# Sixty-four transposes in an attention layer: from TensorE to DMA on planes of 16 bits

## The chip, the cores and the metric

The kernel runs on one core of a Trainium2 chip. Its engines are called PE (TensorE, matrix products), ACT (ScalarE), DVE (VectorE), POOL (GpSimd) and SP (SyncE, which here only issues DMAs). The metric is the device time of one execution in microseconds (us); lower is better.

## The reference

One layer of an encoder on 256 tokens of width 2048: a normalisation, one input projection, two attention branches, sigmoid gates that mix them, an output projection and an MLP. Only the attention and the gates matter here:

```python
proj = jnp.einsum('bsd,dc->bsc', rms_norm(x, norm_mix_pre), w_in)
qa, ka, va, qn, kn, vn, gates = jnp.split(proj, split_at, axis=-1)
# differential attention: 4 heads, two softmaxes of 256 x 256 each
p = softmax(einsum('bqhcd,bkhcd->bhcqk', qa, ka) * scale)      # qa, ka after rope
oa = einsum('bhqk,bkhe->bqhe', p[:, :, 0] - lam * p[:, :, 1], va)
oa = rms_norm(oa, subln_w) * (1 - lambda_init)                 # per head, width 256
# neighbourhood attention: 8 heads, a window on a 4 x 64 grid, with a bias
on = einsum('bhqnw,bnqwhd->bqhd', softmax(q.k * scale + bias), vw)
g_a, g_b = jnp.split(sigmoid(gates), 2, axis=-1)
mixed = g_a * (oa @ w_branch_a) + g_b * (on @ w_branch_b)
```

All data are float32.

## The kernel before

Every float32 operand of a product is kept as two parts, "hi" (a rounded copy, made by ACT) and "lo" (the rest, `x - hi`, made by DVE), and a product is the sum of three: hi x hi, hi x lo, lo x hi (in the weight groups the last with half the columns). `parts` makes such a pair: a cast on ACT, a subtraction on DVE.

The attention part runs through twelve weight groups, q, k and v for each half of the two branches: `qa0, ka0, va0, qa1, ka1, va1, qn0, kn0, vn0, qn1, kn1, vn1` (`wgroup` and `agroup`; the tiles are called `qa_p`, `kn_p`, `vn_p` and so on). Each takes four loads of 1 MB, which SP issues (`load`, three buffers), each with a split into hi and lo. Their sums lie in four PSUM banks (pool `mm`), which a group takes over from the one before: the first product into a bank waits until the bank's old content has been read. For k groups that reading is `halves`: a copy on ACT (`sc_r`), then a sum on DVE (`sc_s`).

After them come the gates: `ga` (eight weights of 1 MB, gate a, first half of the columns), `ba` (four weights, branch a's projection), then `gb`, `bb`, and the same for the second half. `ga` and `ba` use the same four `mm` banks (numbered 1, 2, 3, 7: `ga01`, `ba01` and so on). A bank of `ga` is free once ACT has put its sigmoid into the gate (L906, with a load of the sigmoid's table ahead of the first one).

The attention heads are generators, `diff_head` (d0 to d3) and `na_head` (n0 to n7). They are advanced by a step or two between the loads of the weight groups (`advance`), so that d0 and d1 run beside qa1 to va1, d2 and d3 beside qn0 to vn0, n0 to n3 beside qn1 to vn1, and n4 to n7 beside `ga`. A head's steps: scores and softmax give p, 256 x 256 (tiles `dp`, `np`, 128 partitions x 2 x 256); its transpose as a hi/lo pair (`d_pT`, `n_pT`); the product with v (`do`, `no`). A d head then normalises its rows (`don`) and transposes these too (`dot`), which gives the hi/lo pair `oaT`, the operand of `ba`; an n head casts its product into `onT`, the operand of `bb`. p, its pair and other temporaries live in one ring of seven buffers (`t2k`).

A transpose is a PE instruction of 128x128, four to a PSUM bank, with ACT's cast and DVE's subtraction reading that bank: 16 for `d_pt`, 32 for `n_pt`, 16 for `dot`.

Beside `ga`'s last four weights, `h_sums` prepares sums of `hT` for `gb`: `hf` and `hs0s` to `hs6s` on DVE, their casts on ACT (`hs0`, `hs2`, `hs4`, `hs6`), their subtractions on DVE. `hf` also takes its four tiles from the `t2k` ring.

The order of the instructions on each engine isn't that of the text: a scheduler sorts them by its own estimate of time when the kernel is built (`TC`). On the chip each engine then runs its list strictly in order.

Of the kernel before, what the change touches and what calls it, by code (L numbers as in the profile page):

```python
# [10 lines left out]

F32 = mybir.dt.float32
F32R = mybir.dt.float32r
AF = mybir.ActivationFunctionType
ALU = mybir.AluOpType
AX = mybir.AxisListType

P = 128
D = 2048
T = 256  # L20
# [30 lines left out]
def encoder_layer(ctx: ExitStack, tc: tile.TileContext, a, out):  # L51
    nc = tc.nc
# [18 lines left out]
    def t2k(name, dt=F32):  # L71
        return tmp.tile([P, 2, T], dt, tag="t2k", name=name, bufs=7)

    def bank(name, big=False):
        if big:
            return mm.tile([P, 512], F32, tag="mm", name=name)
        return ms.tile([P, 512], F32, tag="ms", name=name)
# [40 lines left out]
    def split(raw, name, pieces=2, after=(), then=None):  # L118
# [3 lines left out]
        _, nk, cw = (P, len(raw), 512) if listed else raw.shape  # L122
        hi = wp.tile([P, nk, cw], F32R, tag="hi", name=f"{name}_h")
        lo = wp.tile([P, nk, cw], F32R, tag="lo", name=f"{name}_l")
        prev = front if then else ()
# [30 lines left out]
    at = 0  # L156
# [7 lines left out]
    ident = const.tile([P, P], F32, name="ident")  # L164
# [133 lines left out]

    hT = [page([P, 2, 512], F32R, f"hT{i}") for i in range(8)]

    def x_part(k):
# [3 lines left out]
        g = g_pre[:, k : k + 1]  # L305
        i = nc.scalar.activation(d[:, :T], src, AF.Copy, scale=g).ins
        j = nc.vector.scalar_tensor_tensor(  # L307
# [30 lines left out]
    def x_squares(i):  # L338
        for t in range(2):
            j = junk512("jx0").rearrange("p a b -> p (a b)")  # L340
            nc.scalar.activation(
                j, xp[i][:, t], AF.Square, accum_out=ssx[:, t * 4 + i : t * 4 + i + 1]
            )
# [10 lines left out]
    def head_constants():  # L354
# [5 lines left out]
        le = small(2, "le")  # L360
        nc.scalar.activation(le, ls, AF.Exp)
        nc.vector.scalar_tensor_tensor(
# [55 lines left out]
    def parts(dst, at, src):  # L418
        hi, lo = dst
        nc.scalar.copy(hi[at], src)  # L420
        nc.vector.tensor_sub(lo[at], src, hi[at].bitcast(F32))
# [34 lines left out]
    def v_evac(dst):  # L456
        hi, lo = dst

        def evac(t, ps):
            r = rx[:, t : t + 1]  # L460
            nc.scalar.activation(hi[:, t], ps, AF.Copy, scale=r)
            nc.vector.scalar_tensor_tensor(
# [2 lines left out]

        return evac

    def p_transposed(p, name):

        pt = bank(f"{name}_pt")  # L470
        for kt in range(2):
            for t in range(2):
                nc.tensor.transpose(
                    pt[:, kt * T + t * P : kt * T + (t + 1) * P],
                    p[:, t, kt * P : (kt + 1) * P],
                    ident,
                )
        r = [t2k(f"{name}_pT{i}", F32R) for i in range(2)]
        parts(r, slice(None), pt.rearrange("p (k q) -> p k q", k=2))
        return r  # L480

    def diff_head(h, qT, kT, v, hl, sc):
        p = t2k(f"dp{h}")
        for t in range(2):
            s = bank(f"ds{h}{t}")
            for c in range(2):
                product3(
                    s[:, c * T : (c + 1) * T],
                    qT,
                    (slice(None), hl * 2 + c, slice(t * P, (t + 1) * P)),  # L490
                    kT,
                    (slice(None), hl * 2 + c),
                    True,
                    True,
                )
            nb = small(2, f"dnb{h}{t}")
            nc.vector.tensor_reduce(
                nb, s.rearrange("p (c k) -> p c k", c=2), axis=AX.X, op=ALU.max, negate=True
            )
            nbs = small(2, f"dnbs{h}{t}")  # L500
            nc.vector.tensor_scalar_mul(nbs, nb, sc[t])
            e = t2k(f"de{h}{t}")
            z = small(2, f"dz{h}{t}")
            for c in range(2):
                nc.scalar.activation(
                    e[:, c],
                    s[:, c * T : (c + 1) * T],
                    AF.Exp,
                    bias=nbs[:, c : c + 1],
                    scale=sc[t],  # L510
                    accum_out=z[:, c : c + 1],
                )
            rz = small(2, f"drz{h}{t}")
            nc.vector.reciprocal(rz, z)
            nc.vector.tensor_mul(rz[:, 1:2], rz[:, 1:2], lam)
            nc.vector.tensor_scalar_mul(e[:, 1], e[:, 1], rz[:, 1:2])
            nc.vector.scalar_tensor_tensor(
                p[:, t], e[:, 0], rz[:, 0:1], e[:, 1], op0=ALU.mult, op1=ALU.subtract
            )
        yield True  # L520
        pT = p_transposed(p, f"d{h}")
        yield True
        o = bank(f"do{h}")
        for t in range(2):
            for kt in range(2):
                product3(
                    o[:, t * T : (t + 1) * T],
                    pT,
                    (slice(None), kt, slice(t * P, (t + 1) * P)),
                    v,  # L530
                    (slice(None), kt, slice(hl * T, (hl + 1) * T)),
                    kt == 0,
                    kt == 1,
                )
        ss = small(2, f"dss{h}")
        on = t2k(f"don{h}")
        for t in range(2):
            nc.scalar.activation(
                on[:, t], o[:, t * T : (t + 1) * T], AF.Square, accum_out=ss[:, t : t + 1]
            )  # L540
        r = inv_rms(ss, 2 * HD, f"dr{h}")
        for t in range(2):
            nc.vector.tensor_scalar_mul(on[:, t], o[:, t * T : (t + 1) * T], r[:, t : t + 1])
        yield True
        pt = bank(f"dot{h}")
        for eb in range(2):
            for t in range(2):
                nc.tensor.transpose(
                    pt[:, eb * T + t * P : eb * T + (t + 1) * P],
                    on[:, t, eb * P : (eb + 1) * P],  # L550
                    ident,
                )
        ot = page([P, 2, 512], F32R, f"oaT{h}")
        for eb in range(2):
            src = pt[:, eb * T : (eb + 1) * T]
            g = subs[:, eb : eb + 1]
            nc.scalar.activation(ot[:, eb, :T], src, AF.Copy, scale=g)
            nc.vector.scalar_tensor_tensor(
                ot[:, eb, T:], src, g, ot[:, eb, :T].bitcast(F32), op0=ALU.mult, op1=ALU.subtract
            )  # L560
            oT["a", h * 2 + eb] = ot[:, eb]

    def na_head(h, qT, kT, v, hl):
        p = t2k(f"np{h}")
        s = bank(f"ns{h}")
        for t in range(2):
            product3(
                s[:, t * T : (t + 1) * T],
                qT,
                (slice(None), hl, slice(t * P, (t + 1) * P)),  # L570
                kT,
                (slice(None), hl),
                True,
                True,
            )
        b = bias[h // 2][:, h % 2]
        for t in range(2):
            nc.vector.scalar_tensor_tensor(
                p[:, t],
                s[:, t * T : (t + 1) * T],  # L580
                rxs[:, t : t + 1],
                b[:, 2 - 2 * t : 6 - 2 * t].rearrange("p i c -> p (i c)"),
                op0=ALU.mult,
                op1=ALU.add,
            )
        nb = small(2, f"nnb{h}")
        nc.vector.tensor_reduce(nb, p, axis=AX.X, op=ALU.max, negate=True)
        z = small(2, f"nz{h}")
        for t in range(2):
            nc.scalar.activation(  # L590
                p[:, t], p[:, t], AF.Exp, bias=nb[:, t : t + 1], accum_out=z[:, t : t + 1]
            )
        rz = small(2, f"nrz{h}")
        nc.vector.reciprocal(rz, z)
        for t in range(2):
            nc.vector.tensor_scalar_mul(p[:, t], p[:, t], rz[:, t : t + 1])
        yield True
        pT = p_transposed(p, f"n{h}")
        yield True
        o = bank(f"no{h}")  # L600
        for kt in range(2):
            product3(
                o[:, :T],
                v,
                (slice(None), kt, slice(hl * P, (hl + 1) * P)),
                pT,
                (slice(None), kt),
                kt == 0,
                kt == 1,
            )  # L610
        if h % 2 == 0:
            oT["nt", h // 2] = page([P, 2, 512], F32R, f"onT{h}")
        ot = oT["nt", h // 2][:, h % 2]
        nc.scalar.copy(ot[:, :T], o[:, :T])
        nc.vector.tensor_sub(ot[:, T:], o[:, :T], ot[:, :T].bitcast(F32))
        oT["n", h] = ot
# [772 lines left out]
    for g in range(2):  # L1389
        pr = Products(f"p{g}", (1, 2, 3, 7))  # L1390
        pr.in_order = True
        for bi, b in enumerate(blocks[g]):
            end = bi == len(blocks[g]) - 1
            for n, (cg, j, seven) in enumerate(down_steps(g, bi)):
# [42 lines left out]
                for which in range(4):  # L1437
# [4 lines left out]
                    if last:  # L1442
                        bank_, t, half = PLAIN[which]
# [65 lines left out]
```

## Time and profile before

| what | value |
|---|---|
| median of 3 runs | 1339.47 us (1339.23 to 1339.55) |
| the profiled execution | 1339.37 us, its span 1337.6 us |
| PE busy | 1329.0 us, 99% of the span |
| DVE, ACT busy | 1096.8 us (82%), 740.3 us (55%) |
| twelve groups of q, k, v and `ga` | up to about 347 us of the span |

A row of a timeline has the start in us, the duration in us, the engine, the line of the kernel, the operation, `out<-in` by tile names, the PE tile, the elements (partitions x elements) and how many instructions stand together; in brackets the idle time of the engine just before and what ended it. A row by tile or line has the minimum, median and maximum duration in ns, then the first and the last start in us. The granted clock is the share of its full clock that PE was allowed in a stretch. Durations of PE's products overlap, since they are pipelined: the time that one takes from PE is the distance of two starts.

### The profile page before, as it was taken

The page shows a single profiled execution, that of the slowest core. Times are in us where ns is not written, and L with a number is a line of the kernel's source. Part 1 is how long each engine was busy: PE and PEld are TensorE (multiplying, and loading weights), DVE is VectorE, ACT ScalarE, POOL GpSimd, SP SyncE. Part 2 cuts the span into 40 slices and gives each one's busy share as a digit, 9 for nine tenths or more (in the row PEclk, how much of TensorE's full clock was granted, in tenths as well). Part 3 has the DMA queues.
Part 4 walks back from the last instruction along what each step waited for, and adds up shares of the span by engine and source line. Part 5 has one row for each costly group of instructions (what it writes and reads, how often), then busy time and mean ns, then how long its engine had stood idle before and what let it go on. Part 6 is the DMA issues. An engine that isn't in the chain of part 4 may idle for free.

```text
span 1337.6 us, 16286 instructions
## 1 busy us (share of the span) xinstructions
PE 1329.0 (99%) x6305; PEld 1113.4 (83%) x6305; DVE 1096.8 (82%) x1277; ACT 740.3 (55%) x869; POOL 39.4 (3%) x73
## 2 busy tenths in 40 slices
PE   9999999999999999999999999999999999999997
PEld 8888888888888888888888888888888888888886
DVE  7978766667787897885688999999988988898886
ACT  6655554544545555555476666666555555555542
POOL 0000000000000000000100000000000000000000
PEclk9999999999999999999999999999999999999999
DMA  9874655564564656567658677877797998798995
GB/s 354 277 215 161 193 168 176 184 187 157 189 220 172 207 190 207 188 232 254 226 184 277 239 253 273 297 239 245 250 360 287 402 379 311 271 372 330 358 351 207
DMA packets 114125, 335.85 MB, mean 251 GB/s; under 512 B 16768, under 2 KB 17280, under 8 KB 114048
## 3 DMA queue, kind: packets, MB, share of 16 engines
q1 hardware_dynamic: 94368, 265.87, 57.5%
q10 hardware_dynamic: 12960, 43.26, 8.4%
q0 software_dynamic: 6720, 25.69, 4.9%
q8 instruction: 49, 0.80, 0.2%
q14 instruction: 28, 0.23, 0.0%
HBM read 307.01 MB, written 29.61 MB: 252 GB/s over the span
## 4 chain that ended last, share of the span: by engine, by line
PE 75%; issue 21%; DMA 1%; DVE 1%; ACT 1%; POOL 0%; SPq 0%; POOLq 0%; ACTq 0%
PE u L742 25%; PE ga L742 6%; PE gb L742 6%; PE ba L742 3%; PE bb L742 3%; PE y L742 3%; PE qn_p L223 2%; PE ka_p L223 2%; PE kn_p L223 2%; PE qa_p L223 2%; PE ka_p L225 1%; PE qn_p L225 1%; PE kn_p L225 1%; PE vn_p L267 1%; PE vn_p L266 1%
## 5 line engine op out<-in xcount | busy, mean ns | idle before, releaser
L223 PE MATMUL qn_p<-hT,qn_h 128*128 128x512 f32 x128 | 45.9, 400 | 0.0
L223 PE MATMUL kn_p<-hT,kn_h 128*128 128x512 f32 x128 | 45.6, 400 | 0.0
L223 PE MATMUL ka_p<-hT,ka_h 128*128 128x512 f32 x128 | 45.2, 399 | 0.0
L742 PE MATMUL u<-u_2h,h2T 128*128 128x512 f32 x128 | 44.0, 396 | 0.0
L223 PE MATMUL qa_p<-hT,qa_h 128*128 128x512 f32 x128 | 43.6, 399 | 0.3 <-DVE hT L307 0.3
L742 PE MATMUL u<-u_1h,h2T 128*128 128x512 f32 x128 | 43.4, 389 | 0.0
L742 PE MATMUL u<-u_4h,h2T 128*128 128x512 f32 x128 | 43.2, 391 | 0.0
L742 PE MATMUL u<-u_7h,h2T 128*128 128x512 f32 x128 | 41.0, 389 | 0.0
L742 PE MATMUL u<-u_6h,h2T 128*128 128x512 f32 x128 | 41.0, 389 | 0.0
L225 PE MATMUL qn_p<-hT,qn_l 128*128 128x256 f32 x128 | 35.9, 281 | 0.0
L225 PE MATMUL kn_p<-hT,kn_l 128*128 128x256 f32 x128 | 35.7, 280 | 0.0
L225 PE MATMUL ka_p<-hT,ka_l 128*128 128x256 f32 x128 | 35.2, 282 | 0.0
L225 PE MATMUL qa_p<-hT,qa_l 128*128 128x256 f32 x128 | 32.5, 282 | 0.1
L145 DVE TENSOR_TENSOR y_l<-y_w,y_h 128x1024 fp32r<-128x1024 f32 x16 | 19.0, 1222 | 11.9 <-ACT y_h L137 11.9
L223 PEld LDWEIGHTS kn_p<-hT,kn_h 128*128 128x128 f32 x128 | 24.0, 188 | 5.4
L223 PEld LDWEIGHTS qn_p<-hT,qn_h 128*128 128x128 f32 x128 | 24.1, 188 | 5.3
L145 DVE TENSOR_TENSOR kn_l<-kn_w,kn_h 128x1024 fp32r<-128x1024 f32 x16 | 19.0, 1220 | 11.5 <-ACT kn_h L137 11.5
L223 PEld LDWEIGHTS ka_p<-hT,ka_h 128*128 128x128 f32 x128 | 23.9, 188 | 5.3
L742 PEld LDWEIGHTS u<-u_1h,h2T 128*128 128x128 f32 x128 | 24.0, 188 | 5.0
L145 DVE TENSOR_TENSOR vn_l<-vn_w,vn_h 128x1024 fp32r<-128x1024 f32 x16 | 19.0, 1221 | 11.2 <-ACT vn_h L137 11.2
L742 PEld LDWEIGHTS u<-u_7h,h2T 128*128 128x128 f32 x128 | 24.0, 188 | 5.0
L742 PEld LDWEIGHTS u<-u_6h,h2T 128*128 128x128 f32 x128 | 24.0, 188 | 5.0
(1632 smaller groups left out, 4567.5 us busy)
## 6 DMA issues: line engine op xcount, KB each, us to landing
bh<-keeph ACTq DMA_DIRECT2D x30, 512.0 KB, 9.1
bl<-keepl ACTq DMA_DIRECT2D x30, 512.0 KB, 10.6
keeph<-ah POOLq DMA_DIRECT2D x18, 512.0 KB, 3.8
keepl<-al POOLq DMA_DIRECT2D x18, 512.0 KB, 7.1
va_w<-in_w_in SPq DMA_DIRECT2D x8, 1024.0 KB, 5.2
qn_w<-in_w_in SPq DMA_DIRECT2D x8, 1024.0 KB, 5.2
kn_w<-in_w_in SPq DMA_DIRECT2D x8, 1024.0 KB, 5.1
vn_w<-in_w_in SPq DMA_DIRECT2D x8, 1024.0 KB, 5.0
```

The costliest lines, as they stand in the source:

```text
L145: sub = nc.vector.tensor_sub(lo[part], src, hi[part].bitcast(F32)).ins
L223: nc.tensor.matmul(ps[b], hi[:, k % 4, cs], mv, start=(k == 0), stop=False)
L225: nc.tensor.matmul(ps[b][:, :T], lo[:, k % 4, cs], mv[:, :T], start=False, stop=(k == nk - 1))
L266: nc.tensor.matmul(ps[t], sh, hi[:, k % 4], start=(k == 0), stop=False)
L267: nc.tensor.matmul(ps[t], sh, lo[:, k % 4], start=False, stop=False)
L742: ins = nc.tensor.matmul(self.ps[i], st, mv[:, blk], start=i not in self.begun, stop=last and n == 2).ins
```

## The change

The transposes of p and of the normalised rows are no longer PE instructions. `send` copies the 128 x 512 floats on ACT into two planes of 16-bit halves (128 x 1024 elements), and SP issues one DMA that transposes the eight 128 x 128 blocks of 16 bits. `received` joins the halves again by another copy on ACT. 16 such transfers (4 dp, 4 do, 8 np) replace the 64 transposes; 32 copies are new on ACT. The hi/lo pairs and `oaT` are then made from SBUF in place of PSUM. In the transposed tile the token block stands ahead of the key block, hence the changed indices of the products. The copy and the DMA of `send` are issued at the end of the step that makes p or the rows, the joining in the next step. Each transfer takes two (`_s`, `_g`) and each joined p one further tile of the `t2k` ring.

```diff
@@ -465,18 +466,35 @@
 
         return evac
 
-    def p_transposed(p, name):
-
-        pt = bank(f"{name}_pt")
-        for kt in range(2):
-            for t in range(2):
-                nc.tensor.transpose(
-                    pt[:, kt * T + t * P : kt * T + (t + 1) * P],
-                    p[:, t, kt * P : (kt + 1) * P],
-                    ident,
-                )
-        r = [t2k(f"{name}_pT{i}", F32R) for i in range(2)]
-        parts(r, slice(None), pt.rearrange("p (k q) -> p k q", k=2))
+    def send(p, name):
+
+        planes = t2k(f"{name}_s").rearrange("p a b -> p (a b)").bitcast(U16)
+        planes = planes.rearrange("p (t h c) -> p t h c", t=2, h=2)
+        got = t2k(f"{name}_g").rearrange("p a b -> p (a b)").bitcast(U16)
+        nc.scalar.copy(planes, p.bitcast(U16).rearrange("p t (c h) -> p t h c", h=2))
+        nc.sync.dma_start(
+            got.rearrange("p (b q) -> p b q", q=P),
+            planes.rearrange("p t h c -> p (t h c)"),
+            transpose=True,
+        )
+        return got
+
+    def received(got, name):
+
+        r = t2k(name)
+        nc.scalar.copy(
+            r.bitcast(U16).rearrange("p t (c h) -> p t h c", h=2),
+            got.rearrange("p (t h c) -> p t h c", t=2, h=2),
+        )
+        return r.rearrange("p t (k q) -> p t k q", k=2)
+
+    def p_received(got, name):
+
+        pT = received(got, f"{name}_pT")
+        r = [
+            t2k(f"{name}_pT{i}", F32R).rearrange("p t (k q) -> p t k q", k=2) for i in range(2)
+        ]
+        parts(r, slice(None), pT)
         return r
 
     def diff_head(h, qT, kT, v, hl, sc):
@@ -517,8 +535,9 @@
             nc.vector.scalar_tensor_tensor(
                 p[:, t], e[:, 0], rz[:, 0:1], e[:, 1], op0=ALU.mult, op1=ALU.subtract
             )
+        got = send(p, f"dp{h}")
         yield True
-        pT = p_transposed(p, f"d{h}")
+        pT = p_received(got, f"d{h}")
         yield True
         o = bank(f"do{h}")
         for t in range(2):
@@ -526,7 +545,7 @@
                 product3(
                     o[:, t * T : (t + 1) * T],
                     pT,
-                    (slice(None), kt, slice(t * P, (t + 1) * P)),
+                    (slice(None), t, kt),
                     v,
                     (slice(None), kt, slice(hl * T, (hl + 1) * T)),
                     kt == 0,
@@ -541,22 +560,19 @@
         r = inv_rms(ss, 2 * HD, f"dr{h}")
         for t in range(2):
             nc.vector.tensor_scalar_mul(on[:, t], o[:, t * T : (t + 1) * T], r[:, t : t + 1])
+        got = send(on, f"do{h}")
         yield True
-        pt = bank(f"dot{h}")
-        for eb in range(2):
-            for t in range(2):
-                nc.tensor.transpose(
-                    pt[:, eb * T + t * P : eb * T + (t + 1) * P],
-                    on[:, t, eb * P : (eb + 1) * P],
-                    ident,
-                )
+        oT_ = received(got, f"dot{h}")
         ot = page([P, 2, 512], F32R, f"oaT{h}")
         for eb in range(2):
-            src = pt[:, eb * T : (eb + 1) * T]
+            src = oT_[:, :, eb]
             g = subs[:, eb : eb + 1]
-            nc.scalar.activation(ot[:, eb, :T], src, AF.Copy, scale=g)
+            hi, lo = (
+                ot[:, eb, at * T : (at + 1) * T].rearrange("p (t q) -> p t q", t=2) for at in range(2)
+            )
+            nc.scalar.activation(hi, src, AF.Copy, scale=g)
             nc.vector.scalar_tensor_tensor(
-                ot[:, eb, T:], src, g, ot[:, eb, :T].bitcast(F32), op0=ALU.mult, op1=ALU.subtract
+                lo, src, g, hi.bitcast(F32), op0=ALU.mult, op1=ALU.subtract
             )
             oT["a", h * 2 + eb] = ot[:, eb]
 
@@ -594,17 +610,18 @@
         nc.vector.reciprocal(rz, z)
         for t in range(2):
             nc.vector.tensor_scalar_mul(p[:, t], p[:, t], rz[:, t : t + 1])
+        got = send(p, f"np{h}")
         yield True
-        pT = p_transposed(p, f"n{h}")
+        pT = p_received(got, f"n{h}")
         yield True
         o = bank(f"no{h}")
         for kt in range(2):
             product3(
-                o[:, :T],
+                o[:, :T].rearrange("p (t q) -> p t q", t=2),
                 v,
                 (slice(None), kt, slice(hl * P, (hl + 1) * P)),
                 pT,
-                (slice(None), kt),
+                (slice(None), slice(None), kt),
                 kt == 0,
                 kt == 1,
             )
```

The scheduler orders all engines anew. In the changed kernel the lines stand 1 later up to L467 and 17 later behind `na_head` (L906 is L923, L742 is L759). Below, the numbers behind names tell buffers apart.

PE, the end of `ga` and the first products of `ba`, before:

```order
L742 MATMUL ga07_2969<-ga0_7h_3202,hT7_134 128x512
L742 MATMUL ga07_2969<-ga0_7l_3203,hT7_134 128x512
L742 MATMUL ga07_2969<-ga0_7h_3202,hT7_134 128x512 x2
L742 MATMUL ga07_2969<-ga0_7l_3203,hT7_134 128x512
L742 MATMUL ga07_2969<-ga0_7h_3202,hT7_134 128x512
L742 MATMUL ba01_3356<-ba0_0h_3340,oaT0_1232 128x512
```

and in the changed kernel:

```order
L759 MATMUL ga07_2989<-ga0_7h_3218,hT7_134 128x512
L427 MATMUL no6_3222<-n6_pT0_3122,vn10_2218 128x256
L427 MATMUL no7_3232<-n7_pT0_3128,vn10_2218 128x256
L427 MATMUL no6_3222<-n6_pT1_3123,vn10_2218 128x256
L427 MATMUL no6_3222<-n6_pT0_3122,vn11_2219 128x256
L427 MATMUL no6_3222<-n6_pT0_3122,vn10_2218 128x256
L427 MATMUL no6_3222<-n6_pT1_3123,vn10_2218 128x256
L427 MATMUL no6_3222<-n6_pT0_3122,vn11_2219 128x256
L427 MATMUL no7_3232<-n7_pT1_3129,vn10_2218 128x256
L427 MATMUL no7_3232<-n7_pT0_3128,vn11_2219 128x256
L427 MATMUL no7_3232<-n7_pT0_3128,vn10_2218 128x256
L427 MATMUL no7_3232<-n7_pT1_3129,vn10_2218 128x256
```

One more product of no7, and then `ba01`, follow. The products of the last two heads have moved from the middle of `ga` to its end.

ACT at the same place, before (`ga00<-ga01` is the sigmoid that frees the bank of `ga01`):

```order
L817 CAST hs0_3173<-hs0s_3168 128x512
L614 CAST onT6_3213<-no6_3206 128x256
L614 CAST onT6_3213<-no7_3216 128x256
L817 CAST hs2_3233<-hs2s_3228 128x512
L677 CAST ba0_0h_3340<-ba0_0r_3338 128x2048
L817 CAST hs4_3268<-hs4s_3263 128x512
L817 CAST hs6_3303<-hs6s_3298 128x512
L677 CAST ba0_1h_3346<-ba0_1r_3344 128x2048
L906 ACT_TABLE_LOAD
L906 ACTIVATE ga00_2890<-ga01_2948,rx_135 128x512
```

and in the changed kernel:

```order
L421 CAST n7_pT0_3128<-n7_pT_3126 128x512
L694 CAST ba0_2h_3368<-ba0_2r_3366 128x2048
L834 CAST hs0_3189<-hs0s_3184 128x512
L631 CAST onT6_3229<-no6_3222 128x256
L631 CAST onT6_3229<-no7_3232 128x256
L834 CAST hs2_3249<-hs2s_3244 128x512
L834 CAST hs4_3284<-hs4s_3279 128x512
L834 CAST hs6_3319<-hs6s_3314 128x512
L923 ACT_TABLE_LOAD
L923 ACTIVATE ga00_2902<-ga01_2968,rx_135 128x512
```

The casts of the sums stand between the last head's pair and the sigmoids as before, but now directly behind n7's products.

DVE at the same place in the changed kernel (before, `hf` stands between the subtractions of ga's weights 5 and 6):

```order
L846 TENSOR_TENSOR hf6_3311<-hT6_133 128x256 x2
L830 TENSOR_TENSOR hs0s_3184<-hf0_3181 128x128
L829 TENSOR_TENSOR hs0s_3184<-hf0_3181 128x128
L696 TENSOR_TENSOR ba0_2l_3369<-ba0_2r_3366,ba0_2h_3368 128x2048
L831 TENSOR_TENSOR hs0s_3184<-hs0s_3184,hf0_3181 128x128
L832 TENSOR_TENSOR hs0s_3184<-hf0_3181,hs0s_3184 128x128
L829 TENSOR_TENSOR hs2s_3244<-hf2_3241 128x128
L830 TENSOR_TENSOR hs2s_3244<-hf2_3241 128x128
L831 TENSOR_TENSOR hs2s_3244<-hs2s_3244,hf2_3241 128x128
L835 TENSOR_TENSOR hs0_3189<-hs0s_3184,hs0_3189 128x512
```

`hf6`'s tile of the ring is that of `n6_pT1`, which the last no6 product with `n6_pT1` (the sixth of the last twelve) frees; `ba0_2l` has moved in among the sums.

ACT around the casts of vn0's weights, before:

```order
L538 ACTIVATE don3_1895,dss3_1894<-do3_1881 128x256 x2
L137 CAST vn0_0_h_2076<-vn0_0_w_2074 128x1024 x2
L557 ACTIVATE oaT2_1949<-dot2_1944,subs_139 128x256 x2
L137 CAST vn0_1_h_2108<-vn0_1_w_2106 128x1024 x2
L557 ACTIVATE oaT3_1999<-dot3_1994,subs_139 128x256
L291 COPY sc_r_2020<-kn0_p0_1814 128x256
```

and in the changed kernel:

```order
L557 ACTIVATE don3_1905,dss3_1904<-do3_1891 128x256 x2
L138 CAST vn0_0_h_2084<-vn0_0_w_2082 128x1024 x2
L474 COPY do3_s_1914<-don3_1905 128x1024
L485 COPY dot2_1958<-do2_g_1848 128x2x2x256
L573 ACTIVATE oaT2_1960<-dot2_1958,subs_139 128x256 x2
L485 COPY dot3_2005<-do3_g_1915 128x2x2x256
L138 CAST vn0_1_h_2116<-vn0_1_w_2114 128x1024 x2
L573 ACTIVATE oaT3_2007<-dot3_2005,subs_139 128x256 x2
L292 COPY sc_r_2028<-kn0_p0_1820 128x256
```

The copy that joins dot3 has come in ahead of vn0_1's casts and of `sc_r`; it needs the transfer that SP issues once `do3_s` is written. On DVE vn0_1's subtractions and oaT3's stand ahead of `sc_s` too.

More of the change, by code (lines that the diff above doesn't have):

```diff
@@ L13 @@
 F32R = mybir.dt.float32r
+U16 = mybir.dt.uint16
 AF = mybir.ActivationFunctionType
```

## The prediction

> **What bounds the kernel now.** I read the page's busy line first, then the busy time by stretch of the span, then the order of instructions around the places that the change touches, each against the timeline of before.
>
> ```profile
> span 1337.6 us, 16286 instructions
> PE 1329.0 (99%) x6305; PEld 1113.4 (83%) x6305; DVE 1096.8 (82%) x1277; ACT 740.3 (55%) x869; POOL 39.4 (3%) x73
> ...
> 60.00:345.00 285.00, 285.00 (x1552) 246.43 (x1551) 206.31 (x356) 147.76 (x254) 3.08 (x4) 1.00 0.57 180
> ...
> 1330.00:1338.00 8.00, 1.13 (x4) 0.68 (x4) 3.14 (x6) 1.63 (x5) 0.77 (x1) 0.68 0.53 195
> ```
>
> The first two rows are the page's; the other two are stretches of the span (length, then busy time of PE, PEld, DVE, ACT and POOL with their counts, granted clock, DMA share, GB/s). From 60 to 345 us, which holds every step of the change, PE is busy for 285.00 of 285.00 us: it waits for nothing. So a us of work taken from PE there is a us won, and a us in which PE has to wait is a us lost, since no slack stands behind it. ACT is busy for 147.76 of these 285 us (52%), DVE for 206.31 (72%). The profiled run took 1339.4 us, 1.8 us more than its span, and the median of the runs is 1339.47; I work against 1339.4.
>
> **What is removed: 64 transposes on PE.**
>
> ```profile
> L548 PE MATMUL dot<-ident,don x16: 270/272/273, 113.7 to 194.5; 128*128 128x128 f32 x16
> ...
> L473 PE MATMUL d_pt<-ident,dp x16: 270/272/273, 87.3 to 171.0; 128*128 128x128 f32 x16
> ...
> L473 PE MATMUL n_pt<-ident,np x32: 270/272/273, 247.5 to 317.3; 128*128 128x128 f32 x32
> ...
> 113.23 0.28 PE L225 MATMUL ka_p<-hT,ka_l 128*128 128x256 f32 x1
> 113.35 0.40 PE L223 MATMUL ka_p<-hT,ka_h 128*128 128x512 f32 x1
> 113.59 0.28 PE L225 MATMUL ka_p<-hT,ka_l 128*128 128x256 f32 x1
> 113.71 0.60 PE L548 MATMUL dot<-ident,don 128*128 128x128 f32 x4
> 114.06 0.48 PE L223 MATMUL ka_p<-hT,ka_h 128*128 128x512 f32 x1
> 114.38 0.28 PE L225 MATMUL ka_p<-hT,ka_l 128*128 128x256 f32 x1
> ```
>
> A transpose lasts 272 ns, but overlaps its neighbours. The last six rows are the timeline of PE (start, us). What four transposes take is read there from the starts of the 256-wide products: 113.23 to 113.59 is 0.36 us without them, 113.59 to 114.38 is 0.79 with them, so 0.43 to 0.44 for four. 64 of them: 16 x 0.44 = 7.0 us. All lie in the stretch with no waits, so the whole 7.0 us is won, if nothing new waits. The products that use the transposed rows keep their number and sizes. The reads of PSUM by the casts become reads of SBUF of the same sizes; I cost that at nothing, since ACT has 137 us free.
>
> **What is added on ACT: 32 copies of 128x1024 elements of 16 bits.**
>
> ```profile
> L137 ACT CAST vn_h<-vn_w x16: 1043/1050/1057, 188.2 to 279.3; 128x1024 fp32r<-128x1024 f32 x16
> ```
>
> The nearest row with 1024 elements a partition is this cast, 1.05 us. Bounds: half of it if 16 bits go twice as fast, twice if the stride of two elements halves the rate. I take 1.05: 32 x 1.05 = 33.6 us, and ACT goes to 181 of 285 us (64%). As a quantity it is hidden. What counts is order: a "received" copy waits on ACT for its DMA, and everything behind it on ACT waits too.
>
> **What is added on SP: 16 transposing DMAs of 256 KB, in order among the weight loads.** The trace of before has none. The nearest rows (KB each, median us from issue to landing):
>
> ```profile
> vn_w<-in_w_in SPq DMA_DIRECT2D x8, 1024.0 KB, 5.0
> ...
> keeph<-ah POOLq DMA_DIRECT2D x18, 512.0 KB, 3.8
> ...
> xT<-in_xT SPq DMA_DIRECT2D x6, 256.0 KB, 7.8
> ...
> bias<-skew SPq DMA_DIRECT2D x16, 96.0 KB, 4.6
> ```
>
> Call X the time from issue to landing. From below, 3.8 us (512 KB in long runs). From above, the bias rows: their runs are 64 x 4 = 256 bytes, 384 of them to 96 KB; a transpose moves rows of 128 x 2 = 256 bytes, 1024 of them, and at the same time per run lands in 4.6 x 1024/384 = 12.3 us. I take 6.2: the transposing DMA mostly stands behind a 1 MB load (5.0 us) and its own 256 KB at that load's rate take 1.2 us more. The xT row, 7.8, comes from the crowded start of the program.
>
> The Trainium skill ("VectorE: DVE Perf Modes", The three transpose paths) gives 1309 ns for one 128x128 block by the DMA crossbar against 390 ns on TensorE. Eight blocks one after another would be an estimated 10.5 us, near my upper end; by that page the sum would be the rival of slow transfers below. No row of this trace can show it yet.
>
> **Where X costs time: the first product of vn0.** Rows of the timelines of ACT, DVE and PE (start, us):
>
> ```profile
> 188.20 2.00 ACT L137 CAST vn_h<-vn_w 128x1024 fp32r<-128x1024 f32 x2 [3.03 <-PE kn_p L223]
> ...
> 196.60 0.36 ACT L291 COPY sc_r<-kn_p 128x256 f32<-128x256 f32 x1
> ...
> 189.28 2.36 DVE L145 TENSOR_TENSOR vn_l<-vn_w,vn_h 128x1024 fp32r<-128x1024 f32 x2 [1.64 <-ACT vn_h L137]
> 191.56 0.48 DVE L558 SCALAR_TENSOR_TENSOR oaT<-dot,subs,oaT 128x256 fp32r<-128x256 f32 x1
> ...
> 198.09 0.75 DVE L293 TENSOR_TENSOR sc_s<-kn_p,sc_r 128x256 f32<-128x256 f32 x2
> ...
> 200.29 0.40 PE L266 MATMUL vn_p<-vn_h,hT 128*128 128x512 f32 x1
> ```
>
> vn0's product at 200.29 takes the PSUM bank that sc_s at 198.09 frees: 1.8 us to spare. In the new order (the ACT rows in the section on the change) do3's send stands behind vn0_0's casts, and dot3's received copy stands ahead of vn0_1's casts, oaT3 and sc_r. By then PE has some 24 transposes fewer (2.6 us), so vn0_0's casts end at 190.2 - 2.6 = 187.6, the send copy at 188.7, and the DMA lands at 188.7 + X. Then: copy 1.05, vn0_1's casts 2.0, its second subtraction on DVE 1.2, oaT3's two 0.8, sc_s 0.42, and 0.3 for handing over: 5.8 us. PE would like to start at 200.29 - 32 x 0.11 = 196.8. So it waits for 188.7 + X + 5.8 - 196.8 = X - 2.3 us: 3.9 at 6.2, 1.5 at 3.8, 10.0 at 12.3.
>
> Other places where ACT holds a received copy have room at 6.2. The nearest is d0 and d1: from p (87.3, the transposes' first row) to the first product that uses it,
>
> ```profile
> L426 PE MATMUL do<-va,d_pT x48: 280/283/287, 99.5 to 182.4; 128*128 128x256 f32 x48
> ```
>
> lie 12.2 us; two copies take 2.1, cast and subtraction 1.3, and some 2 go behind other casts, so that X up to about 6.8 is free. The loads behind a DMA that SP holds back are early: the cast at 188.20 waited for PE, not for its load.
>
> **Where the order costs time, whatever X is: the first product of ba0.** This is the largest term. Again rows of the three timelines:
>
> ```profile
> 329.80 1.60 PE L426 MATMUL no<-n_pT,vn 128*128 128x256 f32 x12
> ...
> 347.35 0.39 PE L742 MATMUL ga<-ga_7h,hT 128*128 128x512 f32 x1
> 347.58 0.39 PE L742 MATMUL ba<-ba_0h,oaT 128*128 128x512 f32 x1
> ...
> 330.59 0.76 DVE L829 TENSOR_TENSOR hf<-hT 128x256 f32<-128x256 f32 x2 [0.35 <-PE no L426]
> 331.27 0.28 DVE L812 TENSOR_TENSOR hs2s<-hf 128x128 f32<-128x128 f32 x1
> ...
> 334.35 0.69 DVE L818 TENSOR_TENSOR hs<-hs0s,hs 128x512 fp32r<-128x512 f32 x1
> 334.95 0.75 DVE L615 TENSOR_TENSOR onT<-no,onT 128x256 fp32r<-128x256 f32 x2
> ...
> 338.89 2.29 DVE L679 TENSOR_TENSOR ba_0l<-ba_0r,ba_0h 128x2048 fp32r<-128x2048 f32 x1 [0.72 <-ACT ba_0h L677]
> ...
> 331.81 0.62 ACT L817 CAST hs<-hs0s 128x512 fp32r<-128x512 f32 x1
> 332.33 0.64 ACT L614 CAST onT<-no 128x256 fp32r<-128x256 f32 x2
> ...
> 344.31 1.28 ACT L906 ACT_TABLE_LOAD   x1
> 345.61 1.85 ACT L906 ACTIVATE ga<-ga,rx 128x512 f32<-128x512 f32 x3
> ```
>
> ba01, the first product of ba0, takes the bank of ga01, which the first sigmoid frees. Before, the last n products (329.80) end 16 us ahead of ba0, hf and hs follow them, and the table load and sigmoid (344.31, 345.61) come in time: PE goes from ga at 347.35 to ba at 347.58. In the new order the products of no6 and no7 stand last before ba0, and ahead of the sigmoid ACT has hs0, two onT, hs2, hs4 and hs6; DVE's hf6 waits for the last product that reads `n6_pT1`, the sixth of the last twelve: 0.7 us before their end E. From E on, by the rows above: hf6 to 0.1; two hs0s operations (0.2 to 0.28 each) 0.6; ba0_2l 2.9; two more 3.4; cast hs0 4.0; on ACT two onT 4.65, on DVE three hs2s, hs0's subtraction and the last hs2s 5.0; cast hs2 5.65; on DVE two onT 5.8, two hs4s 6.3, hs2's subtraction 7.0, two hs4s 7.5; cast hs4 8.1; on DVE three hs6s 8.2, hs4's subtraction 8.9, last hs6s 9.2; cast hs6 9.8; table load 11.1; sigmoid 11.7. Some eight hand-overs of 0.04 bring it to 12.0 us in which PE has nothing else in its order. Bounds: 10, if hand-overs overlap and ba0_2l comes early, to 13.
>
> **The clock after that wait.** In the last stretch of before, where PE idles, the granted clock is 0.68. If the 8 us after a wait of 12 us run so, it costs 8 x 0.32 = 2.6 us; if not, 0. I take the middle, 1.3. The Trainium skill ("TensorE: Matmul & The Clock Gate", Part 1: The HAM clock gate) says that the array falls to half rate after about 3.4 us idle and returns after about 3.4 us of work; by that the estimate is 1.7 and the sum 0.4 higher, and the 0.68 row agrees in direction.
>
> **The sum.** 1339.4 - 7.0 (transposes) + 12.0 (ba0) + 3.9 (vn0) + 1.3 (clock) = 1349.6, said as 1350.
>
> **Rivals.**
> - Slow transfers, X at 12.3. For it: the runs of 256 bytes in the bias rows. Against: a quarter of a 1 MB load's bytes. vn0 then waits for 10.0; d0 and d1 exceed their 6.8 by 5.5 each, one behind the other on one queue, 11; the pairs of n heads alike, once or twice. 1339.4 - 7.0 + 12.0 + 1.3 + 10.0 + 11 + 11 = 1368, or 1379 with one more pair; about 1373.
> - The other side: PE doesn't wait for the sigmoid at ba0. For it: before, the first sigmoid ended at 346.2, 1.4 us ahead of ba01, and the n heads' data are ready many us before PE takes them up. It decides if hf, hs and sigmoid stand ahead of E by the 12 us that the walk puts behind it; against it, the printed order, in which DVE can't pass hf6. Then 1339.4 - 7.0 + 3.9 = 1336.3, at X = 3.8 1333.9, at X = 7.8 1337.9.
>
> **Chances.** The forecast 0.67, with a range of its own of 1345 (X 3.8, ba0 11, no clock loss: 1339.4 - 7.0 + 11 + 1.5) to 1356 (X near 8, the slower clock, a first wait at d1); slow transfers 0.20; no wait at ba0 0.13. A change of 0.2% (2.7 us) is about what can be told from none: the last case is mostly faster (0.08) and otherwise the same (0.05); the rest, 0.87, is slower. The range leaves out the last case and the worst of the slow one: 1344 to 1376.
>
> **What would show it.** PE: a wait of about 12 us of ba for ACT's L923 and one of X - 2 us of vn_p for DVE's sc_s, and none elsewhere over 1 us; 64 PE transposes gone. The DMA issues: do_g and np_g with their landing time, which is X. The 16-bit copies at about 1.05 us. A wrong prediction would show as PE going from no7's products to ba0 without a gap, or as waits of ka_p, do or kn_p for ACT.

## The result, and the profile after

The changed kernel takes 1349.55 us in the median (1348.71 to 1350.08, 4 runs) against 1339.51 (1339.23 to 1339.70): the ratio is 1.0074, with an interval of 1.0062 to 1.0086. It is 10 us slower. The profiled execution took 1348.71 us, 1.8 more than its span.

The top of its page:

```profile
span 1346.9 us, 16231 instructions
...
PE 1325.6 (98%) x6241; PEld 1108.3 (82%) x6241; DVE 1097.9 (82%) x1277; ACT 774.7 (58%) x901; POOL 39.2 (3%) x73
```

PE has 64 instructions fewer (6241 for 6305) and ACT 32 more, with 34.4 us more of work. PE is less busy and yet the span is 9.3 us longer, so PE now waits. Its waits in the changed kernel (us in all, how often, the longest):

```profile
PE ba L759 <- ACT ga L923: 12.7, 1, 12.7
...
PE vn_p L267 <- DVE sc_s L294: 0.4, 1, 0.4
...
PE p L759 <- DMA bl<-keepl: 0.2, 1, 0.2
```

The first is new and larger than the whole loss, since the removed transposes gave back some of it: ba0's first product waits for the sigmoid that frees ga01's bank. The second is the forecast wait at vn0, but a tenth of its forecast size. The rows left out, with the 2.2 us of x_last near the end as the longest, are in the kernel before too and about as long there. PE's timeline at ba0 shows the wait and what follows it:

```profile
339.76 1.59 PE L427 MATMUL no<-n_pT,vn 128*128 128x256 f32 x12
354.06 0.79 PE L759 MATMUL ba<-ba_0h,oaT 128*128 128x512 f32 x1 [12.70 <-ACT ga L923]
354.65 0.63 PE L759 MATMUL ba<-ba_0l,oaT 128*128 128x512 f32 x1
...
358.17 0.40 PE L759 MATMUL ba<-ba_1l,oaT 128*128 128x512 f32 x1
358.40 0.39 PE L759 MATMUL ba<-ba_1h,oaT 128*128 128x512 f32 x1
```

The twelve products of no6 and no7 end at 341.36 (354.06 - 12.70). From 354.06 to 358.17 PE starts ten products, 0.41 us apart; from there on they are 0.23 apart. Ten at 0.23 would have taken 2.3 us, not 4.1: 1.8 us are lost after the wait. The granted clock (the number ahead of the last two) in stretches of 2 us fits that:

```profile
342.00:344.00 2.00, 0.00 (x0) 0.00 (x0) 2.00 (x6) 0.00 (x0) 0.00 (x0) 1.00 0.48 197
344.00:346.00 2.00, 0.00 (x0) 0.00 (x0) 1.97 (x4) 0.00 (x0) 0.00 (x0) 0.53 0.00 0
...
354.00:356.00 2.00, 1.94 (x5) 1.56 (x6) 0.42 (x1) 2.00 (x5) 0.00 (x0) 0.50 0.00 0
356.00:358.00 2.00, 2.00 (x7) 1.56 (x6) 1.30 (x2) 1.61 (x2) 0.00 (x0) 0.56 0.00 0
358.00:360.00 2.00, 2.00 (x10) 1.62 (x9) 1.06 (x1) 0.00 (x0) 0.00 (x0) 1.00 0.00 0
```

By the means of 0.53 and 0.56 it fell to a half at 344.1, some 2.8 us after PE went idle, and came back at 357.8, some 3.7 us after PE resumed. What ACT and DVE did meanwhile, the links of the chain in their timelines:

```profile
346.04 0.62 ACT L834 CAST hs<-hs0s 128x512 fp32r<-128x512 f32 x1 [4.17 <-DVE hs0s L832]
346.56 0.64 ACT L631 CAST onT<-no 128x256 fp32r<-128x256 f32 x2
347.61 0.62 ACT L834 CAST hs<-hs2s 128x512 fp32r<-128x512 f32 x1 [0.41 <-DVE hs2s L832]
349.81 0.62 ACT L834 CAST hs<-hs4s 128x512 fp32r<-128x512 f32 x1 [1.58 <-DVE hs4s L832]
351.39 0.62 ACT L834 CAST hs<-hs6s 128x512 fp32r<-128x512 f32 x1 [0.96 <-DVE hs6s L832]
352.02 1.28 ACT L923 ACT_TABLE_LOAD   x1
353.32 2.42 ACT L923 ACTIVATE ga<-ga,rx 128x512 f32<-128x512 f32 x4
...
339.51 0.68 DVE L422 TENSOR_TENSOR n_pT<-n_pT,n_pT 128x512 fp32r<-128x512 f32 x1
340.11 2.76 DVE L846 TENSOR_TENSOR hf<-hT 128x256 f32<-128x256 f32 x8
```

ACT is idle between the casts, each time for DVE's next sum: the sigmoid is not waiting for work that it needs, but for work that stands ahead of it in the list.

The transfers themselves, by the tile that a transfer of a d head's rows lands in:

```profile
L475 SPq DMA_TRANSPOSE do_g<-do_s x4: 1232/1232/1234, 111.1 to 188.6; - x4
L485 ACT COPY dot<-do_g x4: 1350/1356/1365, 121.1 to 191.6; 128x1024 uint16<-128x1024 uint16 x4
...
DMA to landing us min/median/max: 2.7/2.7/3.0
```

These four (256 KB each, transposed) are in place 2.7 to 3.0 us after their issue; of the other twelve the fastest took 2.7 too and the slowest 5.9. How long one takes goes with the load ahead of it. SP's timeline shows the transfer that vn0 hangs on, and a later one:

```profile
185.19 0.53 SPq L116 DMA_DIRECT2D vn_w<-in_w_in  x1
188.59 1.23 SPq L475 DMA_TRANSPOSE do_g<-do_s  x1
...
303.93 0.38 SPq L684 DMA_DIRECT2D ga_6r<-in_w_in  x1
305.73 1.23 SPq L475 DMA_TRANSPOSE np_g<-np_s  x1
```

The first of these loads landed 5.4 us after its issue, the second 5.3. The transfers, issued 3.4 and 1.8 us behind them, landed in 3.0 and 4.5 us: each 1.0 us after its load. Eight of the 16 transfers were issued 1.8 to 3.4 us behind a 1 MB load that was still on its way, and all eight landed 0.8 to 1.2 us after that load.

An issue keeps SP for 1.23 us. The joining copy takes 1.36 us (it writes every second 16-bit element), the splitting copy (which reads so) 1.05 as taken.

### The profile page after: what moved, and what is told of

Its sections match the earlier page's. It is cut to its first block, busy times and chain, and to the rows that moved or that the text cites. A ratio compares the mean times of both kernels' runs of the same rounds, so it can differ in the third digit from the quotient of the medians.

```text
span 1346.9 us, 16231 instructions
## 1 busy us (share of the span) xinstructions
PE 1325.6 (98%) x6241; PEld 1108.3 (82%) x6241; DVE 1097.9 (82%) x1277; ACT 774.7 (58%) x901; POOL 39.2 (3%) x73
## 4 chain that ended last, share of the span: by engine, by line
PE 72%; issue 22%; DVE 2%; ACT 2%; DMA 2%; POOL 0%; POOLq 0%; ACTq 0%
PE u L759 25%; PE gb L759 6%; PE ga L759 4%; PE ba L759 3%; PE bb L759 3%; PE y L759 3%; PE qa_p L224 2%; PE qn_p L224 2%; PE ka_p L224 2%; PE kn_p L224 2%; PE qa_p L226 1%; PE qn_p L226 1%; PE ka_p L226 1%; PE vn_p L267 1%; PE vn_p L268 1%
## 5 line engine op out<-in xcount | busy, mean ns | idle before, releaser
L759 PE MATMUL u<-u_2h,h2T 128*128 128x512 f32 x128 | 44.0, 396 | 0.0
L759 PE MATMUL u<-u_1h,h2T 128*128 128x512 f32 x128 | 43.4, 389 | 0.0
L759 PE MATMUL u<-u_4h,h2T 128*128 128x512 f32 x128 | 43.2, 391 | 0.0
L759 PE MATMUL u<-u_7h,h2T 128*128 128x512 f32 x128 | 41.0, 389 | 0.0
L759 PE MATMUL u<-u_6h,h2T 128*128 128x512 f32 x128 | 41.0, 389 | 0.0
L759 PEld LDWEIGHTS u<-u_1h,h2T 128*128 128x128 f32 x128 | 24.0, 188 | 5.0
L224 PEld LDWEIGHTS qa_p<-hT,qa_h 128*128 128x128 f32 x128 | 23.8, 191 | 5.3 <-ACT qa_h L144 0.5
L759 PEld LDWEIGHTS u<-u_7h,h2T 128*128 128x128 f32 x128 | 24.0, 188 | 5.0
L759 PEld LDWEIGHTS u<-u_6h,h2T 128*128 128x128 f32 x128 | 24.0, 188 | 5.0
L759 PEld LDWEIGHTS u<-u_4h,h2T 128*128 128x128 f32 x128 | 24.0, 188 | 4.9
```

Of the source, the lines that this page charges most:

```text
L224: nc.tensor.matmul(ps[b], hi[:, k % 4, cs], mv, start=(k == 0), stop=False)
L759: ins = nc.tensor.matmul(self.ps[i], st, mv[:, blk], start=i not in self.begun, stop=last and n == 2).ins
```

## The experiments

All times are medians, against 1339.5 to 1339.7 for the kernel before on the same chip; ratios are to it.

**1. The sums behind the gate (late_sums).** Does the wait come from the order on ACT?

```diff
             def each(n):
                 advance(2)
-                if n >= 4:
-                    h_sums(SUMMED[n - 4])
...
             if first_one:
                 advance(99)
+                for i in SUMMED:
+                    h_sums(i)
                 temps.close()
```

> Edit: h_sums for gb is written behind the whole of ga instead of beside its last four weights; nothing else. On ACT the table load and the sigmoids then stand ahead of the casts of hs0 to hs6. Theory (the 12.7 us at ba0 are the chain hf, hs0 to hs6, table load, sigmoid behind the last heads): what is left behind no6 is one onT cast 0.4, table load 1.3 and sigmoid 0.6, so PE waits about 2 us at ba0 and too short for the clock to fall: 1349.5 - 10.7 - 1.8 = 1337.0 us. Rival 1 (the transfers and the 32 copies cost the time, by load on ACT and SP): within 1 us of 1349.5. Rival 2 (the wait only moves to gb, which needs hs0 first): ba0 goes through, gb waits for some 10 us, 1346 to 1349.

Measured: 1337.95 us, ratio 0.9988 (0.9979 to 0.9997); 11.6 us less than the whole change, with every transfer and copy kept. Its wait at ba0, and its clock from 343 us on:

```profile
PE ba L759 <- ACT ga L923: 2.8, 1, 2.8
```

```profile
343.00:345.00 2.00, 0.98 (x4) 0.85 (x5) 2.00 (x2) 1.99 (x4) 0.00 (x0) 1.00 0.01 2
...
346.00:347.00 1.00, 1.00 (x4) 0.77 (x3) 1.00 (x5) 0.35 (x1) 0.00 (x0) 0.50 0.69 119
...
349.00:351.00 2.00, 2.00 (x10) 1.62 (x9) 1.91 (x6) 0.63 (x1) 0.00 (x0) 1.00 0.26 104
```

The theory of the order holds, and nothing moved to gb (no such wait). Both rivals fall. One part of the expectation was wrong: a wait of 2.8 us (not 2) did lower the clock, and it fell when PE was already running again, for some 3 us (0.50 from 345.5 to 348.5).

**2. Four tiles of the ring in place of six (back_in_both).** Why do the last heads come so late?

```diff
-        planes = t2k(f"{name}_s").rearrange("p a b -> p (a b)").bitcast(U16)
+        tile = t2k(f"{name}_s")
+        planes = tile.rearrange("p a b -> p (a b)").bitcast(U16)
...
-        got = t2k(f"{name}_g").rearrange("p a b -> p (a b)").bitcast(U16)
+        got = p.rearrange("p a b -> p (a b)").bitcast(U16)
...
-        return got
+        return got, tile
     def received(got, name):
-        r = t2k(name)
+        got, r = got
```

> Edit: the transposing DMA writes back into the tile of p (or of the normalised rows), and the joining copy into the tile of the planes, so that a head takes four tiles of the ring of seven in place of six. Nothing else. The products of no7 then stand 31 rows of PE's order ahead of ba0, some 36 products of 0.23, 8 us. Theory (the ring of seven holds the last heads back, and their chain then holds the sigmoid): the wait at ba0 shrinks from 12.7 by about 8 to 4 us, give or take 2: 1349.5 - 8.5 - 1 = 1340 us, between 1338 and 1342. Rival (the heads are late because of the transfers' own time): the wait stays near 12, 1348 to 1350.

Measured: 1341.15 us, ratio 1.0009 (1.0000 to 1.0018). The waits:

```profile
PE ba L760 <- ACT ga L924: 4.6, 1, 4.6
...
PE p L760 <- DMA bl<-keepl: 1.5, 1, 1.5
```

The wait at ba0 fell from 12.7 to 4.6 us by nothing but two tiles a head. The ring is what pushed the last heads to the end of ga; with six tiles a head and seven in all, one head's tiles must come free before the next head can have its own. Behind this wait the clock was at 0.50 as well, until 350.5, which is 5.5 us after PE resumed.

**3. Both, and the table early (best4).**

```diff
+        if h == 7:
+            warm = small(1, "warm")
+            nc.scalar.activation(warm, z[:, 0:1], AF.Sigmoid)
         got = send(p, f"np{h}")
```

with the edits of 1 and 2.

> Edit: four tiles a head as in back_in_both, h_sums behind ga as in late_sums, and one sigmoid of a single column behind the last exponential of n7, which loads the table early. Theory: nothing stands between ga01 and its sigmoid, PE waits at ba0 for nothing, and what is left is the saving of the transposes: 1339.5 - 6.7 + at most 0.5 at vn0 = 1333 us, 0.5% faster than before. Rival (transposes that were hidden cost PE nothing, and the 16-bit copies do cost): 1339 or more.

Measured: 1332.92 us (1332.67 to 1333.40), ratio 0.9950 (0.9937 to 0.9962): 6.7 us faster than the kernel before, and 16.6 faster than the change as made. ACT puts each sigmoid right behind its bank, and PE passes from ga to ba without a gap; ACT and PE from 336 us on:

```profile
337.80 0.69 ACT L927 ACTIVATE ga<-ga,rx 128x512 f32<-128x512 f32 x1 [0.23 <-PE ga L763]
...
340.09 0.39 PE L763 MATMUL ga<-ga_7h,hT 128*128 128x512 f32 x1
340.32 0.39 PE L763 MATMUL ba<-ba_0h,oaT 128*128 128x512 f32 x1
```

**4. Work that keeps PE going (fill).** Is the loss after the wait the clock's?

```diff
+FILL = 48
...
-            nc.tensor.matmul(
+            last_no[0] = nc.tensor.matmul(
...
                 advance(99)
+                fill = bank("fill")
+                last = last_no[0]
+                for _ in range(FILL):
+                    with tc.issue_after(last):
+                        last = nc.tensor.matmul(
+                            fill, hT[0][:, 0, :P], hT[0][:, 0], start=True, stop=True
+                        ).ins
```

`last_no[0]` holds the latest product that a head has issued, here the last of no7.

> Edit: 48 products of 128x512 into a spare PSUM bank, whose result nobody reads, stand in PE's order between the last product of no7 and the first of ba0; nothing else. They take 48 x 0.228 = 10.9 us of the 12.7 in which PE waits. Theory (1.8 us are lost after the wait because the granted clock falls to 0.50 while PE is idle): the clock stays at 1.00, ba0 starts at the same time as before, and the run is 1.8 us faster, 1347.7. Rival (the clock does not depend on it, or it falls for another reason): 1349.5, with ba0's first ten products at 0.43 each again. If the 48 products ran at half clock themselves, they would take 20 us and the run be 8 us slower.

Measured: 1347.32 us (1346.28 to 1347.80), 2.2 us less than without the 48 products. PE's timeline:

```profile
341.36 11.07 PE L954 MATMUL fill<-hT 128*128 128x512 f32 x48
354.24 0.50 PE L762 MATMUL ba<-ba_0h,oaT 128*128 128x512 f32 x1 [1.82 <-ACT ga L926]
354.58 0.40 PE L762 MATMUL ba<-ba_0l,oaT 128*128 128x512 f32 x1
354.82 0.63 PE L762 MATMUL ba<-ba_0h,oaT 128*128 128x512 f32 x2
```

ba0 starts at nearly the same time (354.24 for 354.06), and from its second product on the starts are 0.23 to 0.24 apart, with the granted clock at 1.00 throughout: useless work on PE made the kernel faster. The 1.8 us behind the wait are the clock's. The other 0.4 of the 2.2 lie within the runs' spread; the profiled run of fill also has no wait of p for the transfer of bl, which the changed kernel has.

**5 and 6. Half of the change (d_only, n_only).** In the first, `na_head` keeps `p_transposed`, and in the second `diff_head` and its `dot` keep their transposes, word for word as before.

> Edit: only the d heads (dp, do: 32 transposes) go by DMA, the n heads keep their transposes on PE. Theory (the wait at ba0 comes from the n heads, and a removed transpose is worth 6.7/64 = 0.105 us of PE): 32 x 0.105 = 3.35 us won, 0.4 lost at vn0, no wait at ba0: 1339.5 - 3.35 + 0.4 = 1336.6 us. Rival (each transfer costs by itself): half of the changed kernel's loss, 1344 to 1345.

> Edit: only the n heads (np: 32 transposes) go by DMA, the d heads keep theirs on PE. Theory: 3.35 us won, ba0 waits for 12 to 13 us with 1.8 for the clock, no wait at vn0: 1339.5 - 3.35 + 12.7 + 1.8 = 1350.7 us, a little slower than the whole change. Rival (each transfer costs by itself): 1344 to 1345.

Measured: d_only 1337.15 us, ratio 0.9982 (0.9974 to 0.9991); n_only 1351.78 us, ratio 1.0091 (1.0077 to 1.0105). The waits of n_only, then of d_only:

```profile
PE ba L775 <- ACT ga L939: 12.7, 1, 12.7
```

```profile
PE vn_p L267 <- DVE sc_s L294: 0.4, 1, 0.4
PE va_p L267 <- DVE rope_s L294: 0.4, 1, 0.4
```

The n heads bring all of the loss, the d heads by DMA are a gain. Both came within 1.1 us of the expected.

**7. Each transpose twice on PE (pe_twice).** The kernel before, with `for kt in (0, 1, 0, 1)` (and the same for `eb`) around the transposes.

> Edit: the kernel before, with each of the 64 transposes issued twice into the same place. Theory (a transpose takes 0.10 to 0.11 us from a PE that never waits): 64 more cost 6.7 to 7.0 us, 1346.2 to 1346.5. Rivals: by their duration of 272 ns 17.4 us, 1357; hidden, 1339.5.

Measured: 1346.57 us, ratio 1.0051 (1.0038 to 1.0064), 6.9 us more for 64 transposes: 0.108 us each.

**8 and 9. Each transfer, each splitting copy twice, in best4.** A `for _ in range(2)` around the DMA of `send`, and in the other around its copy.

> Edit: best4 with each transposing DMA issued twice, the second behind the first into the same place, so that from the first issue to the data in place pass some 5.5 us in place of 2.7. Theory (PE waits for an order, and the transfers have room): no new wait over 1.5 us, 1333 to 1335 us; no7 comes closer to ba0 (12 rows), and ba0 may wait for up to 1 us. Rival (the transfers sit on the path): 16 transfers of 2.7 us more put 5 to 20 us on it, 1338 to 1353.

> Edit: best4 with the copy into the two planes made twice, 16 more copies of 1.05 us on ACT (16.8 us). Theory (ACT has room, only its order counts): 1333 to 1334.5 us, with at most 1 us of new waits, since each second copy delays its transfer by 1.05. Rival (ACT's load is what the change costs): a good part of 16.8 us, 1340 or more.

Measured: with the second DMA 1337.17 us (1335.82 to 1339.03), 4.2 more than best4, above the 1333 to 1335 expected and just under the rival's 1338; with the second copy 1333.41 us, 0.5 more. The waits with the second DMA:

```profile
PE vn_p L267 <- DVE sc_s L294: 1.6, 1, 1.6
...
PE kn_p L224 <- DVE pl_s L294: 0.6, 1, 0.6
PE no L427 <- ACT n_pT L421: 0.4, 2, 0.2
```

So 16.8 us more of work on ACT are hidden, as the sum had it, but a few us more of landing time are not all hidden: vn0 comes first, as forecast, and smaller waits follow at kn1 and the last heads. These waits add up to 2.6 us of the 4.2. By the distance of starts PE loses 1.9 us at vn0, 0.9 at kn1, 0.5 at va1 and some 1.5 in short gaps at the last heads, which covers the whole.

**10. The table alone (late_sums_table).** late_sums with the early sigmoid of best4, six tiles a head.

> Edit: late_sums and one sigmoid of a single column behind n7's last exponential, which loads the sigmoid's table early; a head still takes six tiles of the ring. Theory (late_sums' wait of 2.8 us is onT cast, table load 1.28 and sigmoid behind no6): the wait falls by 1.3 to 1.5 us; a wait of 1.8 us did not lower the clock (fill), one of 2.8 did (late_sums, ten products at 0.43): so the clock stays and 1.5 more are won: 1337.95 - 1.3 - 1.5 = 1335.1 us. Rival (the clock falls after any such wait): 1336.6.

Measured: 1335.05 us, ratio 0.9968 (0.9955 to 0.9980). The wait and the clock behind it:

```profile
PE ba L762 <- ACT ga L926: 1.4, 1, 1.4
```

```profile
342.00:344.00 2.00, 1.35 (x6) 1.13 (x7) 2.00 (x6) 2.00 (x5) 0.00 (x0) 1.00 0.40 162
344.00:346.00 2.00, 2.00 (x11) 1.65 (x10) 2.00 (x4) 0.59 (x2) 0.00 (x0) 1.00 0.00 0
```

1.4 us less of waiting gave 2.9 us less of time: the clock's share went with it. The runs of late_sums spread widely (1335.77 to 1340.43), so the difference of medians alone would be weak evidence; the granted clock, 1.00 here and 0.50 there, shows it directly.

## Why the prediction was right, step by step

- The change's direction and its cause: right. 1350 was forecast, 1349.55 measured, and the place (ba01 behind L923) and the size of the main wait were read from the printed order and from durations of before. Experiments 1 to 3 take that wait away by order alone.
- Transposes, -7.0: 6.9 by experiment 7. The distance of two starts was the right reading; the 272 ns of a row would have given 17.4.
- ba0, +12.0: 12.7. Two errors in the walk partly cancelled. hf6 did not wait for no6: DVE got to the eight hf operations only at 340.11, behind n7's subtraction, and ended them at 342.87, 1.5 us behind E (341.36) and not 0.1. The links behind it took back some 0.8: the first sigmoid ended at 353.94, 12.6 us behind E, where the walk with its hand-overs had 12.0.
- vn0, +3.9: 0.4. This is the term that was mis-sized, by its X. The formula, X - 2.3, comes out: the transfer in question took 3.0 us, which gives 0.7, and PE lost 0.4 by the list of waits and 0.7 by the distance of starts. But X was taken as 6.2, a whole 1 MB load (5.0) and 1.2 for the transfer itself. That a transfer lands behind the load ahead of it was right, as the eight transfers above show. Wrong was that the load's whole time still lies ahead: here it had been issued 3.4 us before, so 2.0 us were left of it, and 1.0 for the transfer. The lower bound of 3.8, from rows of 512 KB, was too high as well; the trace of before has a row of the same 256 KB on SP's queue, from the end of the program, which the prediction does not use:

```profile
out_y<-zw SPq DMA_DIRECT2D x4, 256.0 KB, 2.2
```

- The rival of slow transfers (12.3) is refuted: the slowest of the 16 took 5.9 us. The Trainium skill gives 1309 ns for one 128x128 block ("VectorE: DVE Perf Modes", The three transpose paths); the estimate of 10.5 us, which took eight of them one after another, does not hold for these transfers, whose 2.7 us for eight blocks are 0.34 each, with issue and landing.
- The clock, +1.3: 1.8, shown by experiment 4. The Trainium skill's rule ("TensorE: Matmul & The Clock Gate", Part 1) gave 1.7 and is nearer; the rate of one half agrees (0.50), the return after 3.7 us of work nearly (3.4 there), while the fall came after 2.8 us of idling, sooner than the 3.4 there.
- The copies, hidden: right, by experiment 9, though the joining copy is 1.36 and not 1.05 us.
- The sum with the measured terms, 1339.4 - 6.9 + 12.7 + 0.4 + 1.8, is 1347.4. The profiled run has 1348.7 and the median 1349.55, so that 1 to 2 us are not in these terms, and the closeness of 1350 to the result is in part luck: the 3.5 us too much at vn0 stood for these and for 1.3 too little in the other three terms. What the profiled run has beyond the sum, 1.3 us, can be placed. The list counts a wait from the end of the product before it, which overlaps the next start; by the distance of starts vn0 and ba0 cost some 0.4 us more. So at 1050 us the changed kernel runs 8.4 us behind the kernel before (the same eight products of d030h begin at 1054.8 and at 1046.4). Two places late in the changed kernel add the last 0.9:

```profile
1075.43 0.39 PE L759 MATMUL p<-d050l,bh 128*128 128x512 f32 x1
1076.01 0.50 PE L759 MATMUL p<-d050h,bl 128*128 128x512 f32 x1 [0.19 <-DMA bl<-keepl]
...
1340.71 2.02 PE L1359 MATMUL x_last<-zg,by_rows 128*128 128x256 f32 x4 [2.19 <-ACT by_rows L1356]
```

The wait of p for the transfer of bl costs 0.5 by the distance of starts. And the four products of x_last, behind the wait of 2.2 us that every kernel has, ran at a granted clock of 0.50 almost from their start; in the kernel before, the clock stayed at 1.00 until they were all but done:

```profile
1331.82 1.13 PE L1342 MATMUL x_last<-zg,by_rows 128*128 128x256 f32 x4 [2.19 <-ACT by_rows L1339]
```

That adds some 0.4 to the span. What lies between the profiled run, the fastest of the four, and their median, and the wider spread of the runs (1.4 us against 0.5), stays open; the waits of p on bl vary from 0 to 1.5 us between these kernels and were not tested.
- The rival with no wait at ba0 (1336.3, at X = 3.8 1333.9) was wrong for this order, but its arithmetic is what best4 reached once the order let it: 1332.92.

## What to carry to other kernels

In this kernel, whose main engine hardly ever waits, taking work from it was worth what the distance of two starts said, and nearly everything else was order. So ask of each moved step what stands behind it in its engine's list, and whether an unrelated instruction (here a sigmoid that frees a bank) is now behind a chain that got later. Count the buffers that the new path takes from a shared ring; two tiles a head decided between 1349.5 and 1341. When you price a transfer that stands behind a load, ask how much of the load is left when the transfer is issued. And when PE must wait long, the wait can cost a second time in the clock.

## What the runs showed that I had not expected

- The length of a wait alone did not tell whether the clock falls. At ba0, waits of 1.4 and 1.8 us left it at 1.00 and a wait of 2.8 us brought 0.50, only after PE had resumed. But the wait of 2.2 us before x_last, the same in every kernel, brought 0.50 while the four products behind it ran in the changed kernel and in best4 (2.02 and 1.91 us for them) and left them at 1.13 us in the kernel before, in d_only and in back_in_both.
- Nor was the way back fixed: PE ran at half rate for 3.7 us after the wait of 12.7 us, and for 5.5 us after the shorter wait of 4.6 us in back_in_both.
- Eight 128x128 blocks of 16 bits, SBUF to SBUF, land in 2.7 us at best, with 1.23 us on SP for the issue alone; behind a 1 MB load that is still on its way they land about 1 us after it.
- 48 products that nobody reads made the kernel 2.2 us faster.
